# 96 instead of 128 token slots for each expert of a top-2-of-8 mixture

## The chip, the cores and the metric

The kernel runs on one core of one Trainium2 chip. The core has a matrix engine (PE in the profile, its weight loads in a row of their own, PEld), a vector engine (DVE), a scalar engine (ACT), a general engine (POOL) and 16 DMA engines that are fed by queues, here nearly all by that of SyncE (SP). The metric is device time in microseconds (us) of one launch, the median of several runs. Lower is better.

## What is computed

Two transformer layers over 256 latent tokens and 256 context tokens of width 1024. Layer 0 has retention and attention heads side by side and a dense feed-forward; layer 1 has latent attention and then, for the latent tokens alone, a top-2-of-8 mixture of experts. Only the mixture matters here:

```
t = h.reshape(b * n, d)                                     # 256 tokens, 1024 wide
logits = t @ router                                         # 8 experts
top_v, top_i = lax.top_k(logits, 2)
top_w = softmax(top_v)
gates = sum(one_hot(top_i, 8) * top_w[..., None], axis=1)   # two nonzeros a token
for e in range(8):
    out += gates[:, e:e+1] * ((silu(t @ w1[e]) * (t @ w3[e])) @ w2[e])   # w1, w3: 1024x3584, w2: 3584x1024
```

The reference multiplies all tokens with all experts. With the reference's inputs the router sends 65, 57, 65, 59, 82, 57, 65 and 62 tokens to the eight experts (counted on a CPU from the reference itself).

## The kernel before

All weights are f32 in HBM. For precision an operand is split into two parts of the matrix engine's f32r format, high and low, and a product is made of three matmuls: high times high, low times high, high times low. The split of a weight unit (128 x 2048 values, 1 MB) takes one ACT copy into a tile `uH` (line 103) and one DVE subtraction into a tile `uL` (line 104); both kinds have two buffers. The f32 originals come by DMA into a ring of some dozen 8 KB places (`uraw`, `xp`, `h0`, `a0`, `xn`, `raw`, ...), which the profile shows under those names.

Layer 0 and the attention of layer 1 take the first 820 us. Of the attention's tiles the rows below name `mk` and `mq`, plain f32 operands of a score product with 96 rows, `krx`, which is transposed in blocks of 96 columns, and `sil`, 32 columns of weights for the conditioning. Then `route` (one call for each of the two token tiles) computes norm, router logits, ranks, and for every token its slot at each of its experts (`pos`). `select` writes `S`, a 0/1 matrix of 128 tokens by 2 experts x 128 slots, by comparing `pos` with `iota`. `moe(0)` then does everything for the slots 0 to 127 of every expert:

- gather (`gather_step`, line 1589): for each pair of experts and each of four pairs of K tiles, eight matmuls with the tokens `xnH`, `xnL` as weights and `S` as the stream of 2 x 128 columns; then norm scale and shift (`mhf`, line 1603), then a split into `xe`, of 1024 x 128 for each expert. The gather of the next pair stands among the products of the odd expert before it.
- first products (line 1708): for each expert and each of seven column groups j of 512, `w1` and `w3` in two units each. Weights of a matmul are a 128 x 128 block of `xe` (K by slots), the stream is 512 columns of `uH` or `uL`. 48 matmuls a group.
- `ma` = silu times product (lines 1727, 1728), four transposes (line 1626) and a split into `aa`, slots in columns.
- second product (line 1631): blocks of `aa` as weights, 512 columns of `w2` as stream, 24 matmuls a group, summed over all j in two PSUM banks.
- at the end of an expert the gate and a split make `y` (line 1672), and `scatter` adds it to the token stream `rx` by the transpose `ST` of `S` (line 1686).

After `moe(0)` the largest token count of an expert is read into a register, and if it is over 128, `moe(1)` does the same for slots 128 to 255. It is not entered here. Within an engine the order of the instructions is set by a list scheduler that runs when the kernel is built; only calls in `keep_in_program_order` keep their written order.

Of the kernel before, what the change touches and what calls it, by code (L numbers as in the profile page):

```python
# [8 lines left out]
F32 = mybir.dt.float32  # L9
# [7 lines left out]
P = 128  # L17
# [6 lines left out]
NJ = ED // 512  # L24
MAGIC = float(0x5F3759DF)
# [3 lines left out]
class Split:  # L29
    """an operand in two float32r parts: H(k, cols) + L(k, cols), each [128, cols]"""  # L30
# [14 lines left out]
class SplitRow:  # L45
    """one column per K tile, the same for all tokens"""
# [12 lines left out]
def hybrid_kernel(ctx: ExitStack, tc: tile.TileContext, i, out):  # L59
# [3 lines left out]
    # ------------------------------------------------------------- pools  # L63
# [22 lines left out]
    # ------------------------------------------------------------- weight units of at most 1 MB  # L86
# [35 lines left out]
    def unit_rows(o, X, wh, wl, k0, kn, ktiles, ts_):  # L122
        """o [128 tok, n] += sum over the unit's K tiles of X[k, tok]^T w[k]"""
        for k in range(kn):
            mm(o, X.H(k0 + k, ts_), wh[:, k, :], k0 + k == 0, False)
            mm(o, X.L(k0 + k, ts_), wh[:, k, :], False, False)
        for k in range(kn):
            mm(o, X.H(k0 + k, ts_), wl[:, k, :], False, k0 + k == ktiles - 1)

    def rows_gemm(X, w, ktiles, c0, cn, toks, tags, kmax=4, w0=0):  # L130
        """psum[t] [128 tok, cn] = sum_k X[k, t]^T w[k, c0:c0+cn]"""
# [8 lines left out]
    def rows_pieces(X, w, c0, toks, evac):  # L140
        """one unit of all K tiles, 256 columns, as one piece per token tile"""
        ws = []

        def piece(t):
            if not ws:
                ws.extend(split_unit(w_src(w, 0, KD, c0, 256), (KD, 256)))
            ps = psum("mm")
            unit_rows(ps[:, :256], X, *ws, 0, KD, KD, tok(t))
            evac(t, ps)

        return [(24 * 256, lambda t=t: piece(t)) for t in toks]
# [5 lines left out]
    def block_cols(o, wh, wl, bs, X, cs):  # L157
        """o [128 features, tokens cs]"""
# [6 lines left out]
    def interleave(*lists):  # L165
        """emits lists of (cost, piece) side by side, each spread over the whole"""
# [9 lines left out]
    # ------------------------------------------------------------- helpers  # L176
    def rstd(ms, n, scale=None):
        """1/sqrt(scale*ms + EPS), [P, n] fp32"""
# [24 lines left out]
    def table(f):  # L203
        """the table of a function of ScalarE, ahead of its first use"""
# [9 lines left out]
    def bcast_into(t, reps):  # L214
        """vectors on every partition, each repeated r times"""
# [19 lines left out]
    # ------------------------------------------------------------- adaLN parameters  # L235
    class Ada:
        """columns 2048 r .. 2048 r + 2048; row 32 j + s of the result holds chunk j of stream s"""
# [66 lines left out]
    # ------------------------------------------------------------- norm, modulation, transposition  # L304
    def norm_rows(xr, pool, junk=None, tag="xn", act=()):
        """rows / rms(rows): two [128, D], in place if there is only room for junk"""
# [36 lines left out]
    # ------------------------------------------------------------- softmax attention, one head and query tile at a time  # L343
    def softmax_rows(ps, nk, scale, pool, sums, col, bufs=3):
        """exp(scale (s - max)) in a [128, nk] tile, its sum in sums[:, col]"""
# [8 lines left out]
    # ============================================================= start: streams, vectors, first modulation  # L354
    sil = const.tile([P, KD, 32], F32, tag="sil", name="sil")
    nc.gpsimd.memset(sil, 0.0)
    # the table of this function serves the first norms as well
# [32 lines left out]
    # silu(c), silu(c_ctx) as 32-wide stationary blocks per K tile (columns 0, 1 used)  # L390
# [4 lines left out]
    # ============================================================= layer 0  # L395
    # tiles of 8 KB that the parts after each other take over one by one
# [12 lines left out]
    # the first modulation streams through slots that later hold other things; part q of it is all that K tiles  # L409
    # 2 q and 2 q + 1 of the modulated rows need: row 32 j + s holds shift (j < 2) or 1 + scale of K tile 2 q + j % 2  # L410
# [54 lines left out]
    # ---- GQA query projection, K tile by K tile as the modulated rows appear  # L465
# [48 lines left out]
    # ---- constants of the attention parts: distances (3 x 384), rotary tables, gains  # L514
# [11 lines left out]
    # values: the two parts side by side, in the order high, low for the first key head and low, high for the second  # L526
# [22 lines left out]
    # queries, later values, of two token tiles each  # L549
# [7 lines left out]
    def gqa_pre(s):  # L557
        """normalised and rotated queries and keys; per head, both parts below each other"""
# [30 lines left out]
    # ---- GQA attention, two heads at a time  # L589
    # operand of the output projection: K tile 4 + g holds head g of both key heads, K tile hp two retention heads  # L590
# [47 lines left out]
    # ---- first stretch: gates and retention values with the GQA heads among them  # L638
# [8 lines left out]
    def rv_evac(u):  # L647
        def evac(t, ps):
            """less their mean: the group norm's mean is then zero"""
# [13 lines left out]
    def cols_chunks(w, c0, evacs):  # L663
        """a unit of 256 features, per 128 of them a list of pieces"""
# [52 lines left out]
    # queries of a token tile make room for its values  # L717
# [4 lines left out]
    # ---- retention in quadratic form, two heads at a time, transposed: [2 x 64 dims, 512 tokens]  # L722
# [5 lines left out]
    def ret_masks(hp):  # L728
        """decay by distance, within a stream (both directions, two at distance 0) and from latent to context tokens"""
# [57 lines left out]
    def ret_norm(hp):  # L787
        """group norm over each head: its scale goes into the gate"""
# [17 lines left out]
    # ---- output projection, column half by column half; K tiles of the GQA heads first  # L806
# [30 lines left out]
    # ---- second stretch: retention heads among the next heads' projections  # L837
# [54 lines left out]
    # the latent stream's norm under the context stream's last products  # L892
# [10 lines left out]
    # ---- SwiGLU, in three parts of the hidden width  # L903
# [34 lines left out]
    def ffn_down(part, s):  # L938
        """both column halves for one stream"""
# [10 lines left out]
    for part in range(2):  # L950
        A = new_A()
        f0, nf = PARTS[part]
        for b0 in range(0, nf, 2):
            if part == 0 and b0 == 0:
                # the latent stream first, while the context stream is still being normalised
# [20 lines left out]
    # ---- last part: latent stream first; layer 1 starts on it under the context stream  # L976
# [7 lines left out]
    def blk(n, s=1):  # L984
        """two blocks of one stream: the first, then the second product"""
# [36 lines left out]
    # keys and values of the two streams, queries (the first two take over what the latent stream's hidden rows leave)  # L1022
# [3 lines left out]
    def lora_T(rows, n, gname, X):  # L1026
        """rows transposed, times the gain"""
# [9 lines left out]
    def lora(ps, n):  # L1037
        """rms-normalised rows of ps[t][:, :n]"""
# [15 lines left out]
    def rope_rows(o, sincos, nh):  # L1054
        """o = o * cos + swapped(o) * sin; last axis 32"""
# [10 lines left out]
    def rope_keys(s):  # L1066
        """shared rotary keys of one stream"""
# [25 lines left out]
    def kv_rows(pp, s, tt, kr_, rs2=None):  # L1093
        """rs2: the factor of the rows of CK, where it is still to be applied, and its square"""
# [39 lines left out]
    def q_rows(pp, t):  # L1134
# [15 lines left out]
        # the gains of both sides of the plain part  # L1150
# [21 lines left out]
    # what the shift of the context stream adds to its keys and values  # L1172
# [39 lines left out]
    # ---- last products of the context stream; its norm is applied after the projection  # L1212
# [73 lines left out]
    # ============================================================= layer 1: latent attention  # L1286
# [18 lines left out]
    def mla_attend(t, hp, between):  # L1305
        """values of two heads side by side: [2 x 64 dims, 2 x 128 queries], of which the diagonal blocks count"""
# [17 lines left out]
        # 1 / sum of every query on all partitions  # L1324
# [18 lines left out]
    def w_out_gated(c):  # L1343
        """one column half of w_out times the gate of its columns"""
# [31 lines left out]
    iota = const.tile([P, 2, P], F32, tag="iota", name="iota")  # L1376
    nc.sync.dma_start(iota, bass.AP(tensor=i["iota"].tensor, offset=i["iota"].offset, ap=[[0, P], [P, 2], [1, P]]))
# [5 lines left out]
    def route(t, also=lambda n: None):  # L1383
        """the second norm of one token tile, applied after the router's products; also: what fills its waits"""
# [24 lines left out]
        # rank of every expert; equal logits in index order  # L1409
# [11 lines left out]
        # the slot of every token at each of its experts; others get a slot that no column has  # L1421
# [12 lines left out]
    def select(S, half, e, t):  # L1434
        """columns of the slots of two experts"""
        ins = DVE.tensor_tensor(S[:, t, :, :], iota[:, half, :].unsqueeze(1).to_broadcast([P, 2, P]),
                                pos[:, t, e:e + 2].unsqueeze(2).to_broadcast([P, 2, P]), op=ALU.is_equal)
# [3 lines left out]
    def gather_mm(ps, S, kp, ts):  # L1441
        for kk in range(2):
            o = ps[:, 256 * kk:256 * kk + 256]
# [8 lines left out]
    def gather_first(kp, tag):  # L1452
        """what the first token tile gives the first two experts, before the second tile is routed"""
# [13 lines left out]
    S0 = modp.tile([P, 2, 2, P], F32R, tag="adab", name="S0")  # L1467
# [27 lines left out]
    # the first expert's first weights are split, and what the first token tile gives is gathered, in the waits of the  # L1495
    # routing: quarters (part, unit, quarter) and column pairs by place
# [25 lines left out]
    # ============================================================= experts  # L1522
    mo = ctx.enter_context(tc.tile_pool(name="mo", bufs=1))
    # room that the first expert does not need yet takes weights as well
# [7 lines left out]
    def weights():  # L1532
        """softmax over the two largest logits, as weights of all experts"""
# [22 lines left out]
    def count():  # L1556
        """the largest number of tokens of an expert"""
# [254 lines left out]
```

## Time and profile before

| | |
|---|---|
| timed runs | 1838.48, 1840.38, 1842.13 us, median 1840.38 |
| profiled execution | span 1837.4 us from first to last instruction; no other time is recorded for it |
| mixture of experts | from about 841 us (first product) to 1830 us |
| busy share of the span | PE 98%, PEld 80%, DVE 76%, ACT 61%, DMA 74% |

PE busy is not PE at its peak: matmuls overlap in the record (one of 512 columns is recorded as 390 ns long, but the next one starts 227 ns after it). So the pace of PE is read from starts, or from the length of a run of matmuls, and not from the mean duration. A group row has its busy time, the mean duration of one in ns, and the idle time of the engine just before its instructions with what ended it. A timeline row has start, length, and the count of equal instructions that follow each other.

### The profile page before, as it was taken

Reading aid. Unit: us, or ns where it says so; the run is one execution under the profiler, and the core shown is the slowest. Engines: PE = TensorE matmul, PEld = TensorE weight load, DVE = VectorE, ACT = ScalarE, POOL = GpSimd, SP = SyncE. Lnnn points to the kernel's source line nnn. Section 1 sums busy time; section 2 is a strip of 40 time slices with the busy share of each in tenths; the row PEclk is TensorE's granted clock in tenths of the full one; section 3 lists DMA queues with packets and bytes.
Section 4 is the critical chain, followed back from the end, with each engine's and each line's share of the span. In section 5 each row is a group of like instructions: output and inputs, shape, how many; then the busy total and the mean of one; then the engine's idle time right before and its main releaser. Section 6 shows DMA issues by size and latency. Waiting matters only on the chain.

```text
span 1837.4 us, 23898 instructions
## 1 busy us (share of the span) xinstructions
PE 1793.4 (98%) x9410; PEld 1465.7 (80%) x9410; DVE 1398.4 (76%) x1739; ACT 1124.5 (61%) x1189; POOL 14.2 (1%) x24
## 2 busy tenths in 40 slices
PE   6999999999999999999999999999999999999997
PEld 5778668878779998677888888878878888788786
DVE  4787677334335677788889889898898888898987
ACT  4686543322223454567777877777777777777775
POOL 0000000000000000020000000000000000000000
PEclk9999999999999999999999999999999999999999
DMA  8444442343344566958998999999999999999992
GB/s 284 162 138 132 169 114 93 101 147 109 126 161 151 173 199 209 341 210 311 358 361 323 363 364 355 360 343 351 363 342 370 372 345 336 351 371 367 351 371 79
DMA packets 228729, 483.42 MB, mean 263 GB/s; under 512 B 11013, under 2 KB 65626, under 8 KB 223490
## 3 DMA queue, kind: packets, MB, share of 16 engines
q1 hardware_dynamic: 228416, 481.70, 74.0%
q8 instruction: 76, 1.25, 0.3%
q14 instruction: 43, 0.35, 0.1%
q10 hardware_dynamic: 194, 0.12, 0.0%
HBM read 480.74 MB, written 1.05 MB: 262 GB/s over the span
## 4 chain that ended last, share of the span: by engine, by line
PE 87%; DVE 7%; ACT 2%; DMA 2%; issue 1%; ACTq 0%; DVEq 0%
PE ps L84 81%; PE ps L212 4%; DVE uL L104 3%; PE ps L257 2%; DMA uraw<-in_l_w_in_dram 1%; ACT uH L103 1%; DVE rx L1686 0%; DVE y L104 0%; DMA xn<-in_l_exp_w_dram 0%; DMA rx<-in_x_dram 0%; PE ps L428 0%; DVE rst L193 0%; DVE yg L1672 0%; ACT st L103 0%; DVE stf L761 0%
## 5 line engine op out<-in xcount | busy, mean ns | idle before, releaser
L84 PE MATMUL ps<-uH,xe 128*128 128x512 f32 x1792 | 449.9, 392 | 1.2 <-ACT xe L103 0.9
L84 PEld LDWEIGHTS ps<-uH,xe 128*128 128x128 f32 x1792 | 334.0, 188 | 72.2 <-ACT uH L103 1.3
L104 DVE TENSOR_TENSOR uL<-uraw,uH 128x2048 fp32r<-128x2048 f32 (+3 forms) x126 | 276.2, 2193 | 136.8 <-ACT uH L103 128.9
L103 ACT CAST uH<-uraw 128x2048 fp32r<-128x2048 f32 (+3 forms) x126 | 231.1, 1835 | 205.5 <-PE ps L84 164.7
L84 PE MATMUL ps<-uL,xe 128*128 128x512 f32 x896 | 244.9, 393 | 5.6 <-DVE uL L104 5.5
L104 DVE TENSOR_TENSOR uL<-h,uH 128x2048 fp32r<-128x2048 f32 x95 | 217.3, 2290 | 23.2 <-ACT uH L103 21.0
L84 PE MATMUL ps<-uH,aa 128*128 128x512 f32 x896 | 222.4, 390 | 0.0
L103 ACT CAST uH<-h 128x2048 fp32r<-128x2048 f32 x95 | 181.8, 1916 | 59.7 <-PE ps L84 49.3
L84 PEld LDWEIGHTS ps<-uL,xe 128*128 128x128 f32 x896 | 165.7, 188 | 45.8 <-DVE uL L104 12.8
L84 PEld LDWEIGHTS ps<-uH,aa 128*128 128x128 f32 x896 | 168.1, 188 | 35.5 <-issue 0.5
L84 PE MATMUL ps<-h,uH 128*128 128x256 f32 (+1 forms) x1008 | 176.7, 327 | 0.0
L84 PEld LDWEIGHTS ps<-h,uH 128*128 128x128 f32 x1008 | 150.9, 190 | 21.9 <-issue 3.2
L104 DVE TENSOR_TENSOR uL<-a,uH 128x2048 fp32r<-128x2048 f32 x60 | 137.3, 2290 | 17.2 <-ACT uH L103 13.8
L104 DVE TENSOR_TENSOR uL<-raw,uH 128x2048 fp32r<-128x2048 f32 (+1 forms) x60 | 135.2, 2253 | 15.0 <-ACT uH L103 13.7
L103 ACT CAST uH<-raw 128x2048 fp32r<-128x2048 f32 (+1 forms) x60 | 113.2, 1887 | 36.7 <-PE ps L84 33.9
L103 ACT CAST uH<-a 128x2048 fp32r<-128x2048 f32 x60 | 114.8, 1916 | 33.3 <-PE ps L84 33.3
L84 PE MATMUL ps<-uL,aa 128*128 128x512 f32 x448 | 123.7, 397 | 0.0
L84 PEld LDWEIGHTS ps<-uL,aa 128*128 128x128 f32 x448 | 81.5, 188 | 15.5 <-DVE uL L104 0.5
L84 PE MATMUL ps<-h,uL 128*128 128x256 f32 (+1 forms) x504 | 92.6, 326 | 0.0
L84 PE MATMUL ps<-uH,a 128*128 128x512 f32 x352 | 88.2, 391 | 1.1 <-ACT uH L103 1.1
L104 DVE TENSOR_TENSOR uL<-xp,uH 128x2048 fp32r<-128x2048 f32 (+1 forms) x34 | 76.9, 2262 | 11.9 <-ACT uH L103 9.0
L84 PEld LDWEIGHTS ps<-h,uL 128*128 128x128 f32 x504 | 76.9, 190 | 7.8
(383 smaller groups left out, 2385.7 us busy)
## 6 DMA issues: line engine op xcount, KB each, us to landing
h<-in_l_exp_w_dram SPq DMA_DIRECT2D x94, 1024.0 KB
uraw<-in_l_exp_w_dram SPq DMA_DIRECT2D x60, 1024.0 KB
a<-in_l_exp_w_dram SPq DMA_DIRECT2D x60, 1024.0 KB
raw<-in_l_exp_w_dram SPq DMA_DIRECT2D x58, 1024.0 KB
uraw<-in_l_ffn_w_dram SPq DMA_DIRECT2D x38, 1024.0 KB
uraw<-in_l_ada_w_dram SPq DMA_DIRECT2D x34, 1024.0 KB
xp<-in_l_exp_w_dram SPq DMA_DIRECT2D x30, 1024.0 KB
xn<-in_l_exp_w_dram SPq DMA_DIRECT2D x30, 1024.0 KB
```

The source lines that it names most:

```text
L84: PE.matmul(o, l, r, start=start, stop=stop)
L103: h = ACT.copy(H, src)
L104: l = DVE.tensor_sub(L, src, H.bitcast(F32))
L212: PE.transpose(o, in_, ident[:in_.shape[0], :in_.shape[0]])
L257: PE.matmul(self.ps[32 * j:32 * j + 32, :], sil[:, self.k, :], raw[:, 512 * j:512 * j + 512], start=(self.k == 0), stop=(self.k == KD - 1) ...
```

## The change

Each expert has `CAP` = 96 slots. `S` has 2 x 96 columns, `xe` and `aa` have 96 columns a block, `ma`, `y` and `ST` have 96 partitions, and all products of an expert write 96 PSUM partitions. `moe(1)` now serves slots 96 to 191 and is entered if an expert has more than 96 tokens, and inside that branch a third copy, `moe(2)`, serves the rest. The table `iota` is filled with -1 beyond 255. Matmul count, streams of the weights, DMAs and splits of the weights are the same.

```diff
+CAP = 96
-    iota = const.tile([P, 2, P], F32, tag="iota", name="iota")
-    nc.sync.dma_start(iota, bass.AP(tensor=i["iota"].tensor, offset=i["iota"].offset, ap=[[0, P], [P, 2], [1, P]]))
+    iota = const.tile([P, 3 * CAP], F32, tag="iota", name="iota")
+    nc.gpsimd.memset(iota[:, 2 * P:], -1.0)
+    bcast_into(iota, [(i["iota"], 1, 2 * P)])
...
-        ins = DVE.tensor_tensor(S[:, t, :, :], iota[:, half, :].unsqueeze(1).to_broadcast([P, 2, P]),
-                                pos[:, t, e:e + 2].unsqueeze(2).to_broadcast([P, 2, P]), op=ALU.is_equal)
+        slots = iota[:, CAP * half:CAP * half + CAP]
+        ins = DVE.tensor_tensor(S[:, t, :, :], slots.unsqueeze(1).to_broadcast([P, 2, CAP]),
+                                pos[:, t, e:e + 2].unsqueeze(2).to_broadcast([P, 2, CAP]), op=ALU.is_equal)
...
-            o = ps[:, 256 * kk:256 * kk + 256]
+            o = ps[:, 2 * CAP * kk:2 * CAP * kk + 2 * CAP]
...
-                xe[e + ee] = xp.tile([P, 2, KD, P], F32R, tag=("a1", "a3", "h3")[(e + ee) % 3], name=nm("xe"))
+                xe[e + ee] = xp.tile([P, 2, KD, CAP], F32R, tag=("a1", "a3", "h3")[(e + ee) % 3], name=nm("xe"))
...
-                transpose(tp[:, tok(b)], a[:, tok(b)])
-            aa = mo.tile([P, 2, 4, P], F32R, tag="aa", bufs=2, name=nm("aa"))
-            split_to(aa[:, 0, :, :], aa[:, 1, :, :], v3(tp[:, :], 4))
+                transpose(tp[:, CAP * b:CAP * b + CAP], a[:, tok(b)])
+            aa = mo.tile([P, 2, 4, CAP], F32R, tag="aa", bufs=2, name=nm("aa"))
+            split_to(aa[:, 0, :, :], aa[:, 1, :, :], v3(tp[:, :4 * CAP], 4))
...
-                        mm(yps[ch], aa[:, 0, b, :], wh[:, k, cs], j == 0 and b == 0, False)
-                        mm(yps[ch], aa[:, 1, b, :], wh[:, k, cs], False, False)
+                        mm(yps[ch][:CAP, :], aa[:, 0, b, :], wh[:, k, cs], j == 0 and b == 0, False)
+                        mm(yps[ch][:CAP, :], aa[:, 1, b, :], wh[:, k, cs], False, False)
...
-                        unit_rows(ps, XE, wh, wl, k0, 4, KD, tok(0))
+                        unit_rows(ps[:CAP, :], XE, wh, wl, k0, 4, KD, slice(0, CAP))
...
-    with tc.If(cm > P):
+    with tc.If(cm > CAP):
         moe(1)
+        with tc.If(cm > 2 * CAP):
+            moe(2)
```

The scheduler keeps the order at most places and moves the gather by some rows. On PE, near the start of the second expert, where the first expert's results are scattered (`ps` is PSUM, `S` against `xnH` and `xnL` the gather, the numbers tell tiles apart), eight gather matmuls stood together, of which these are the last two:

```order
L84 MATMUL ps_9173<-S_9047,xnH 128x256
L84 MATMUL ps_9173<-S_9047,xnL 128x256
L84 MATMUL ps_9052<-uL_9056,xe_7968 128x512 x2
L84 MATMUL ps_9021<-y_8975,ST_8089 128x512 x2
L84 MATMUL ps_9052<-uL_9056,xe_7968 128x512 x2
L84 MATMUL ps_9052<-uH_9073,xe_7968 128x512 x8
```

After the change three of the eight stand there, of which these are the last two, and the other five 72 matmuls later:

```order
L85 MATMUL ps_9174<-S_9048,xnL 128x192
L85 MATMUL ps_9174<-S_9048,xnH 128x192
L85 MATMUL ps_9053<-uL_9057,xe_7969 96x512 x3
L85 MATMUL ps_9022<-y_8976,ST_8090 128x512 x2
L85 MATMUL ps_9053<-uL_9057,xe_7969 96x512
L85 MATMUL ps_9053<-uH_9074,xe_7969 96x512 x8
```

On DVE the splits that follow that gather step stood ahead of a weight split and of the split of `aa`:

```order
L104 TENSOR_TENSOR uL_9158<-xp_1561_9155,uH_9157 128x2048
L104 TENSOR_TENSOR xe_9050<-mhf_9182,xe_9050 128x256
L104 TENSOR_TENSOR xe_9051<-mhf_9182,xe_9051 128x256
L104 TENSOR_TENSOR uL_9193<-h_1567_9190,uH_9192 128x2048
L104 TENSOR_TENSOR aa_9152<-ps_9147,aa_9152 128x512
```

and now stand two weight splits later:

```order
L105 TENSOR_TENSOR uL_9159<-xp_1561_9156,uH_9158 128x2048
L105 TENSOR_TENSOR uL_9194<-h_1567_9191,uH_9193 128x2048
L105 TENSOR_TENSOR aa_9153<-ps_9148,aa_9153 128x384
L105 TENSOR_TENSOR uL_9212<-h_1570_9209,uH_9211 128x2048
L105 TENSOR_TENSOR xe_9051<-mhf_9183,xe_9051 128x192
L105 TENSOR_TENSOR xe_9052<-mhf_9183,xe_9052 128x192
```

The rows of DVE at the end of an expert (`yg`, `y`, `rx` among the weight splits) keep their order.

## Rows read from the trace of the kernel before

**Rows 1.** Busy time of each engine by stretch: us, then PE, PEld, DVE, ACT, POOL
```profile
900.00:1000.00 100.00, 100.00 (x457) 82.50 (x456) 91.67 (x59) 74.90 (x52) 0.00 (x0) 1.00 0.95 347
1300.00:1400.00 100.00, 98.94 (x447) 80.77 (x446) 89.16 (x55) 72.37 (x51) 0.00 (x0) 1.00 0.98 357
1700.00:1800.00 100.00, 98.99 (x443) 80.77 (x442) 90.11 (x54) 72.45 (x48) 0.00 (x0) 1.00 0.97 354
```
**Rows 2.** Waits between 900 and 1838 us: who for whom, us in total, times, longest
```profile
ACT uH L103 <- PE ps L84: 165.3, 236, 1.5
DVE uL L104 <- ACT uH L103: 78.8, 161, 1.4
PEld ps L84 <- DVE uL L104: 13.0, 19, 1.0
```
**Rows 3.** PE's groups from 841 us on, by form
```profile
L84 PE MATMUL ps<-uH,xe 128*128 128x512 f32 x1792 | 449.9, 392 | 1.2 <-ACT xe L103 0.9 <-DVE xe L104 0.3
L84 PE MATMUL ps<-uL,xe 128*128 128x512 f32 x896 | 244.9, 393 | 5.6 <-DVE uL L104 5.5
L84 PE MATMUL ps<-uH,aa 128*128 128x512 f32 x896 | 222.4, 390 | 0.0
L84 PE MATMUL ps<-uL,aa 128*128 128x512 f32 x448 | 123.7, 397 | 0.0
L212 PE MATMUL ps<-ident,ma 128*128 128x128 f32 x224 | 34.0, 272 | 0.0
L84 PE MATMUL ps<-y,ST 128*128 128x512 f32 x64 | 23.4, 412 | 1.5 <-ACT y L103 1.0 <-DVE y L104 0.5
```
**Rows 4.** Timeline of PE in a steady stretch: start us, us, instruction, count
```profile
1302.41 1.98 PE L84 MATMUL ps<-uH,xe 128*128 128x512 f32 x8
1304.22 1.07 PE L84 MATMUL ps<-uL,xe 128*128 128x512 f32 x4
1305.13 1.98 PE L84 MATMUL ps<-uH,aa 128*128 128x512 f32 x8
```
**Rows 5.** Timeline of PE and PEld in the first gather
```profile
832.88 0.97 PEld L84 LDWEIGHTS ps<-routS,tT 128*128 128x128 f32 x8
...
835.05 0.28 PE L84 MATMUL ps<-S,xnH 128*128 128x256 f32 x1
...
835.41 0.28 PE L84 MATMUL ps<-S,xnL 128*128 128x256 f32 x1
```
**Rows 6.** Tiles xe, ST, mk, S, krx, sil: duration ns min/median/max, first and last start, forms
```profile
L84 PEld LDWEIGHTS ps<-uH,xe x1792: 186/188/193, 841.8 to 1812.5; 128*128 128x128 f32 x200
L84 PE MATMUL ps<-y,ST x64: 387/392/505, 976.5 to 1829.1; 128*128 128x512 f32 x64
L84 PEld LDWEIGHTS ps<-mk,mq x64: 186/190/246, 764.7 to 816.0; 96*128 96x128 f32 x64
L84 PEld LDWEIGHTS ps<-S,xnH x64: 186/188/192, 832.3 to 1526.5; 128*128 128x128 f32 x64
L212 PEld LDWEIGHTS ps<-ident,S x16: 138/139/223, 833.7 to 1561.6; 128*128 128x128 f32 x16
L212 PEld LDWEIGHTS ps<-ident,krx x48: 122/126/129, 690.7 to 767.4; 128*96 128x96 f32 x48
L257 PEld LDWEIGHTS ps<-uraw,sil x240: 105/108/111, 73.8 to 783.5; 128*32 128x32 f32 x120
```
**Rows 7.** Timeline of PE, plain f32 matmuls of the attention
```profile
764.33 0.60 PE L212 MATMUL ps<-ident,krx 128*96 128x128 f32 x4
764.77 1.03 PE L84 MATMUL ps<-mk,mq 96*128 96x256 f32 x4
```
**Rows 8.** DVE's and ACT's instructions on tiles that shrink, as in 6
```profile
L103 ACT CAST xe<-mhf x32: 392/406/422, 841.3 to 1531.1; 128x256 fp32r<-128x256 f32 x32
L104 DVE TENSOR_TENSOR xe<-mhf,xe x32: 415/419/426, 842.1 to 1531.6; 128x256 fp32r<-128x256 f32 x32
L104 DVE TENSOR_TENSOR aa<-ps,aa x56: 678/684/692, 859.6 to 1817.8; 128x512 fp32r<-128x512 f32 x56
L1601 DVE TENSOR_SCALAR mhf<-ps,s,sh x4: 532/535/538, 840.8 to 842.5; 128x256 f32<-128x256 f32 x4
```
**Rows 9.** Timeline of PE at the end of the third expert
```profile
1219.93 0.39 PE L84 MATMUL ps<-y,ST 128*128 128x512 f32 x1
1220.77 1.21 PE L84 MATMUL ps<-uL,xe 128*128 128x512 f32 x4 [0.45 <-DVE uL L104]
```

More of the change, by code (lines that the diff above doesn't have):

```diff
@@ L1466, in hybrid_kernel @@
     sh2 = mod_shift(mod_T(row1), 2, "sh2_1")
-    S0 = modp.tile([P, 2, 2, P], F32R, tag="adab", name="S0")
+    S0 = modp.tile([P, 2, 2, CAP], F32R, tag="adab", name="S0")
     pairs = [(t, hp) for t in range(2) for hp in range(4)]
@@ L1572, in gather_begin @@
             else:
-                Ss[e] = modp.tile([P, 2, 2, P], F32R, tag="adab", name=nm("S"))
+                Ss[e] = modp.tile([P, 2, 2, CAP], F32R, tag="adab", name=nm("S"))
                 for t in range(2):
@@ L1582, in gather_S @@
                 for t in range(2):
-                    transpose(tp[:, tok(2 * ee + t)], Ss[e][:, t, ee, :].bitcast(F32))
+                    transpose(tp[:CAP, tok(2 * ee + t)], Ss[e][:, t, ee, :].bitcast(F32))
             for ee in range(2):
-                s = mo.tile([P, 256], F32R, tag="ST", bufs=4, name=nm("ST"))
-                ACT.copy(s, tp[:, 256 * ee:256 * ee + 256])
+                s = mo.tile([CAP, 256], F32R, tag="ST", bufs=4, name=nm("ST"))
+                ACT.copy(s, tp[:CAP, 256 * ee:256 * ee + 256])
                 STs[e + ee] = s
@@ L1598, in gather_step @@
                 k = 2 * kp + kk
-                o = ps[:, 256 * kk:256 * kk + 256]
+                o = ps[:, 2 * CAP * kk:2 * CAP * kk + 2 * CAP]
                 if tag and kk:
@@ L1606, in split @@
                 x_ = xe[e + ee]
-                split_to(x_[:, 0, 2 * kp:2 * kp + 2, :], x_[:, 1, 2 * kp:2 * kp + 2, :], hf[:, :, tok(ee)], pin)
+                split_to(x_[:, 0, 2 * kp:2 * kp + 2, :], x_[:, 1, 2 * kp:2 * kp + 2, :], hf[:, :, CAP * ee:CAP * ee + CAP], pin)
             split(0)
@@ L1616, in hf_tile @@
                 if kp % 2 == 0:
-                    spare.append(mo.tile([P, 2, 2, 256], F32, tag="aa", bufs=2, name=nm("mhf")))
+                    spare.append(mo.tile([P, 2, 2, 2 * CAP], F32, tag="aa", bufs=2, name=nm("mhf")))
                 return spare[-1][:, kp % 2, :, :]
-            return mo.tile([P, 2, 256], F32, tag="hf", name=nm("mhf"))
+            return mo.tile([P, 2, 2 * CAP], F32, tag="hf", name=nm("mhf"))
         spare, seconds = [], []
@@ L1646, in second @@
                         b = 2 * u + k
-                        mm(yps[ch], aa[:, 0, b, :], wl[:, k, cs], False, j == NJ - 1 and b == 3)
+                        mm(yps[ch][:CAP, :], aa[:, 0, b, :], wl[:, k, cs], False, j == NJ - 1 and b == 3)
         def second_last(e, j, aa, yps):
-            y = mo.tile([P, 2, D], F32R, tag="y", name=nm("y"))
+            y = mo.tile([CAP, 2, D], F32R, tag="y", name=nm("y"))
             for ch in range(2):
@@ L1656, in second_last @@
                     for b in range(n):
-                        mm(yps[ch], aa[:, 0, b0 + b, :], wh[:, b, :], False, False)
-                        mm(yps[ch], aa[:, 1, b0 + b, :], wh[:, b, :], False, False)
+                        mm(yps[ch][:CAP, :], aa[:, 0, b0 + b, :], wh[:, b, :], False, False)
+                        mm(yps[ch][:CAP, :], aa[:, 1, b0 + b, :], wh[:, b, :], False, False)
                     for b in range(n):
-                        mm(yps[ch], aa[:, 0, b0 + b, :], wl[:, b, :], False, b0 + b == 3)
+                        mm(yps[ch][:CAP, :], aa[:, 0, b0 + b, :], wl[:, b, :], False, b0 + b == 3)
                 y_parts(yps, (ch,), y)
@@ L1667, in y_parts @@
             if y is None:
-                y = mo.tile([P, 2, D], F32R, tag="y", name=nm("y"))
+                y = mo.tile([CAP, 2, D], F32R, tag="y", name=nm("y"))
             for ch in chs:
                 cs = slice(512 * ch, 512 * ch + 512)
-                g = mo.tile([P, 512], F32, tag="hf", name=nm("yg"))
-                DVE.tensor_mul(g, yps[ch], g2[ch])
+                g = mo.tile([CAP, 512], F32, tag="hf", name=nm("yg"))
+                DVE.tensor_mul(g, yps[ch][:CAP, :], g2[ch][:CAP, :])
                 split_to(y[:, 0, cs], y[:, 1, cs], g)
@@ L1725, in moe @@
                     pp.append(ps)
-                a = mo.tile([P, 512], F32, tag="a", name=nm("ma"))
-                tc.keep_in_program_order(ACT.activation(a, pp[0], AF.Silu))
-                DVE.tensor_mul(a, a, pp[1])
+                a = mo.tile([CAP, 512], F32, tag="a", name=nm("ma"))
+                tc.keep_in_program_order(ACT.activation(a, pp[0][:CAP, :], AF.Silu))
+                DVE.tensor_mul(a, a, pp[1][:CAP, :])
                 if e == 0 and j == 0:
```

## The prediction

> **What bounds the kernel now.** I read the windows first. In the mixture of experts PE is busy 99 to 100% of every stretch, at a granted clock of 1.00 (of 2.4 GHz), while DVE stands at 88 to 92% and ACT at 72 to 75% [rows 1]. DMA is also at 95 to 98% of its time, so the waits have to say which of the two binds. ACT waits 165 us for PE to give up `uH` buffers and DVE 79 us for ACT; PE's own loads wait 13 us for `uL` [rows 2], and no wait for a DMA is near that size. The stage is bound by PE, so the question is what a matmul with 96 instead of 128 columns of weights costs.
>
> PE's work there is 4032 expert products (1792 + 896 + 896 + 448) with 512 columns of stream each, 224 transposes of `ma`, 64 scatter matmuls [rows 3] and 128 gather matmuls. In a steady stretch twelve products go from 1302.41 to 1305.13 us [rows 4], that is 2.72 / 12 = 227 ns each. So the products take 4032 x 0.227 = 915 us of the 987 us from the first product's load at 841.8 to the last scatter at 1829.1 [rows 6]. Of the rest, some 20 us are waits, most at the ends of experts, where DVE falls behind by its extra work: there a product starts 0.84 us after the scatter matmul ahead of it, not 0.23 [rows 9].
>
> **What sets 227 ns.** 512 columns at 2.4 GHz are 213.3 ns, so 13.3 ns are over. Gather matmuls, with 256 columns, follow each other at (835.41 - 835.05) / 3 = 120 ns [rows 5], which is 106.7 + 13.3. The charge is thus one for each matmul, and not for each column of the stream; there is one weight load for each matmul. Plain f32 matmuls with the same kind of load (190 ns long, against 188 for the split operands [rows 6]) stream at half the rate: four with 256 columns take 1.03 us, the last of them 0.38, so (1.03 - 0.38) / 3 = 217 ns [rows 7] against 213.3 for two cycles a column. There the charge is 3 ns or less. I read this as a load that runs beside the stream, but takes some of its cycles when the stream runs at the full rate. A load gets shorter with its columns: 139 to 126 ns for transposes from 128 to 96 columns, 190 to 108 for plain f32 from 128 to 32 [rows 6]. So I take the charge to go with the columns of weights: 13.3 x 96/128 = 10.0 ns, a pace of 223.3 ns.
>
> The Trainium skill (TensorE: Matmul & The Clock Gate, section Back-to-back issue gap) gives an isolated matmul N / 2.4 + 2.5 ns, 216 ns for 512 columns, with no term for the columns of weights. The trace has 227, so that charge is not the page's. By the page's form, a charge that the weights' width does not change, products would gain nothing; that is the second case below.
>
> **The change part by part.**
>
> Products: 4032 x 3.3 ns = 13.4 us less, on the path, since PE binds. Bounds: 0 if the charge is fixed; on the other side the third case below. More than 13.4 is excluded as long as a load remains that is charged at all by its columns.
>
> Gather: 64 columns less of stream in 128 matmuls. The stream alone would give 80 + 13 = 93 ns; loads of 128 columns with hardly any stream go at (0.97 - 0.19) / 7 = 111 ns [rows 5], and the gather's weights keep 128 columns. I take 111: 128 x (120 - 111) = 1.2 us less. Bounds: 3.5 us less at 93 ns; and since no split matmul under 256 columns stands in the trace, the nearest row on the other side is plain f32, 0.85 ns a column [rows 7], 163 ns for 192 columns, 5.5 us more. I take the former, because 256 columns are far faster than that row.
>
> Transposes of `ma`: weights are 128 columns as before, the stream is 96 columns instead of 128. Now four transposes go at about 108 ns; 111 by the load. 224 x 3 ns = 0.7 us more; bound 0. The 16 transposes of `S` keep their 128 columns of stream.
>
> DVE and ACT: on DVE the split of `aa` takes 684 ns for 512 columns and that of `xe` 419 for 256 [rows 8], so 1.04 ns a column; 384 columns take some 551, 192 some 352; 56 x 0.13 + 32 x 0.07 = 9.7 us of DVE, about as much on ACT. Almost all of it lies beside PE. It counts only where DVE is behind, at the ends of seven experts: the burst there (`yg`, `y`, `aa`, `rx`) gets 0.13 us shorter, with the two `S` of a pair 0.27, about 1.3 us in all. Against it, PE comes to the same buffers sooner: 1.5% of some 12 us a burst, 0.18 us an expert, 1.3 us. I take 0 for the two, bounds -1.3 and +1.3. Without the cover of PE's products all 9.7 us would show.
>
> Before the first product the path runs over `S`, the gather and three `mhf` of 535 ns on DVE [rows 8]: 25% fewer columns, some 0.07 us each, and one split: 0.35 us less.
>
> The moved rows of gather and splits: the gather is done tens of microseconds before its expert needs `xe`, so a place 72 matmuls later costs nothing by itself. A step that stands among products adds the same 8 matmuls to PE wherever it stands. If DVE were late there, a `uL` would come late by at most the two splits that moved, 0.7 us, for three pairs 2 us; I take 0.
>
> DMA: the same bytes. If products get 1.5% faster the rate goes from about 357 to 362 GB/s over such windows; the busy share of 0.98 [rows 1] is no full queue, since no engine waits for it. The iota table's memset and its DMA stand far ahead of their use. The second branch is not entered, and the third lies inside it.
>
> Sum: -13.4 - 1.2 + 0.7 + 0 - 0.35 = -14.2 us. The profiled execution has a span of 1837.4, so 1823.2; the median of the timed runs is 3.0 us over that span, so **1826.2 us**, 0.8% faster. For this case alone the range is 1821 to 1831.
>
> **The rivals.**
>
> *The charge does not depend on the weights' width* (for: it is the same for 256 and 512 columns, and would be as well if it were the exchange of weights; against: plain f32 shows next to none with the same load). Then -0.8 us remain: 1839.5, no change that can be told.
>
> *The narrower load is dearer* (slower). The place is each of the 4032 products. 13.3 ns are 32 cycles for 128 columns, four columns a cycle. If that were a fast way of loading that only full 128 columns get, 96 columns would take 96 cycles, 40 ns, and a product 253 ns: 4032 x 26.7 = 108 us more, 1947. It decides from 1.1 ns a product on: at 228.1 ns the time is 0.2% over the median, with the other terms at -0.8. Against it: the recorded load of split operands is as long as plain f32's (188 and 190 ns [rows 6]), and loads of 96 columns stand in the trace, beside the stream as ever, with four transposes in 0.60 us [rows 7].
>
> The Trainium skill (same page, section Weight-path perf modes) says that fast weight load is on when the number of weights is 128 and the type is not FP32, and speaks so against this change. No run here shows whether f32r counts as FP32 there; the equal loads speak for it.
>
> *The gather at 192 columns falls to a slower rate*: at 163 ns for 192 columns the sum is -7.5 us instead of -14.2, 1832.9; at the whole 217 ns of that row for 256 columns, 128 x 97 = 12.4 us more, 1839.8.
>
> *The change doesn't do what it says*: an expert with more than 96 tokens lets `moe(1)` run, some 985 us more. The counts of the reference's inputs end at 82, and the branch for over 128 stayed untaken, so this has under 1%.
>
> **How the numbers follow.** The charge goes with the width, and all else as summed: 53%, 1821 to 1831. The charge is fixed: 25%, 1836 to 1842. The gather is slower: 10%, 1833 to 1852 by either charge. The load is dearer: 8%, from 1844 on. It falls by more than its share, below 1820: 4%. A change of 0.2%, 3.7 us, is about what a measurement of this kernel can tell from none. Faster than 1836.7: 53 + 4, half of the gather's 10, and a tenth of the fixed one's 25, 0.64. Slower than 1844.1: the dearer load, 2 of the gather's, and some of the fixed one's with bad moves, 0.13. The same: 0.23. The range 1820 to 1843 leaves out the dearer load, the far end of the gather and the below-1820 case, some 17%.
>
> **What would show it.** Starts in a steady stretch: twelve products in 2.68 us (right), 2.72 (fixed), 3.04 (dearer). PEld's loads of `xe` and `aa` shorter than 188 ns by 13 to 27. Eight gather matmuls in a row at 111 ns (93, 163). The transposes of `ma` four in about 0.44 us to the next start. PE's busy share unchanged, its waits for `uL` of the same size. If the time falls with products at 227 ns, the gain is from waits, and my reading of the charge is wrong.

## The result, and the profile after

The changed kernel takes 1850.22 us (median of 4 runs, 1848.94 to 1852.48), the kernel before 1840.0 in the same comparison (4 runs, 1838.48 to 1842.13). The ratio is 1.0059, with a 95% interval from 1.0047 to 1.0072: slower by 10 us, where 14 us faster were predicted, and outside the range. The profiled execution has a span of 1847.8 us.

PE is the bound as before. These are the windows that answer to [rows 1] (busy us of PE, PEld, DVE, ACT, POOL, then the granted clock, DMA share and GB/s):

```profile
900.00:1000.00 100.00, 99.92 (x446) 70.06 (x445) 89.38 (x57) 71.56 (x49) 0.00 (x0) 1.00 0.94 341
1300.00:1400.00 100.00, 98.87 (x446) 68.94 (x445) 86.60 (x56) 71.81 (x54) 0.00 (x0) 1.00 0.96 345
1700.00:1800.00 100.00, 98.85 (x440) 68.53 (x439) 87.51 (x55) 70.34 (x48) 0.00 (x0) 1.00 0.98 360
```

PE is as busy as it was, at the same clock of 1.00, and gets through fewer instructions in each of the three (446, 446 and 440, before 457, 447 and 443), while its loads take 69 to 70 us of a stretch, not 81 to 82. The waits that answer to [rows 2], from 900 us on, show who is late:

```profile
ACT uH L104 <- PE ps L85: 196.3, 246, 1.9
DVE uL L105 <- ACT uH L104: 95.8, 180, 1.3
...
PEld ps L85 <- DVE uL L105: 8.9, 15, 0.9
```

ACT and DVE wait longer for PE (196 and 96 us, before 165 and 79), and PE's loads less for them (8.9, before 13.0). So PE has become slower at the same work. The timeline of PE in a steady stretch answers to [rows 4]:

```profile
1306.20 2.03 PE L85 MATMUL ps<-uH,xe 128*96 128x512 f32 x8
1308.07 1.09 PE L85 MATMUL ps<-uL,xe 128*96 128x512 f32 x4
1309.00 2.00 PE L85 MATMUL ps<-uH,xe 128*96 128x512 f32 x8
1310.84 1.09 PE L85 MATMUL ps<-uL,xe 128*96 128x512 f32 x4
1311.76 0.63 PE L85 MATMUL ps<-uH,aa 128*96 128x512 f32 x2
```

Twelve products take 2.80 and then 2.76 us, before 2.72. Over all gaps under 260 ns from the start of a product to that of the next product or scatter matmul, from 870 us on, the mean is 231.7 ns (3767 gaps), before 227.5 (3739). This mean is called the pace below. PE's groups by form, from 843 us on, answer to [rows 3]; the loads come from the same view of the whole span:

```profile
L85 PE MATMUL ps<-uH,xe 128*96 128x512 f32 x1792 | 458.8, 396 | 3.2 <-ACT uH L104 3.2
...
L213 PE MATMUL ps<-ident,ma 96*128 96x96 f32 x224 | 28.3, 245 | 0.0
```
```profile
L85 PEld LDWEIGHTS ps<-uH,xe 128*96 128x96 f32 x1792 | 286.2, 162 | 125.5 <-ACT uH L104 5.5
...
L213 PEld LDWEIGHTS ps<-ident,ma 96*128 96x128 f32 x224 | 25.4, 140 | 9.5
```

The recorded load of a product did get shorter, 162 for 188 ns, and yet products follow each other more slowly. Transposes of `ma` went the other way: their load is as long as before (140, before 139), and they follow each other at 83 ns instead of 108.

Two things lie ahead of the steady part. The last matmul of the router starts 1.9 us later than before (836.50, not 834.64 us), with the work up to there unchanged but for the table of `iota`; some 500 matmuls in, in layer 0, it is late already (74.3 us, before 72.0). This point moves from profile to profile (834.63 to 838.14 us in e1 to e8, e10, e13 and e14 below), and I put it down to no part of the change. (In e9, e11 and e12 it lies at 841.45, 837.10 and 839.99; their unused tile moves tiles of layer 0 too.) And in this profile twelve gather matmuls and the first eight products run at half the clock:

```profile
843.79 0.41 PE L85 MATMUL ps<-S,xnL 128*128 128x192 f32 x1
844.00 3.62 PE L85 MATMUL ps<-uH,xe 128*96 128x512 f32 x8
847.42 1.25 PE L85 MATMUL ps<-uL,xe 128*96 128x512 f32 x4
```

The products start 427 ns apart, which is 512 columns at 1.2 GHz, and the gather matmuls 213 ns instead of 111; the granted clock of 842 to 850 us is 0.64. PE had waited ahead of this, 0.82 us for `uH` among the gather's matmuls. The products cost 8 x 0.2 = 1.6 us in this profile; the slow gather matmuls fall into a time in which PE waits for `xe` at the full clock (in e1 1.1 us from the last of them to the first product). It comes and goes: of the kernels below, e3 and e5 have the same order and a wait of the same length there (1.11 us from one start to the next), and e3 shows no such product, e5 ten.

From the 25th product to the last scatter matmul it is 989.4 us (851.28 to 1840.70), before 981.1 (847.98 to 1829.08): 8.3 more. The pace gives 4008 x 4.15 = 16.6, transposes 224 x -25 = -5.6, the 96 gather matmuls in that part 96 x -12.6 = -1.2; what is left, -1.5, I take to be shorter waits, since ACT and DVE have more time; no run shows it by itself.

### The profile page after: what moved, and what is told of

It is laid out like the page before. It is cut to its first block, busy times and chain, and to the rows that moved or that the text cites. A ratio compares the mean times of both kernels' runs of the same rounds, so it can differ in the third digit from the quotient of the medians.

```text
span 1847.8 us, 23895 instructions
## 1 busy us (share of the span) xinstructions
PE 1803.3 (98%) x9410; PEld 1356.4 (73%) x9410; DVE 1389.7 (75%) x1739; ACT 1115.3 (60%) x1189; POOL 14.2 (1%) x25
## 4 chain that ended last, share of the span: by engine, by line
PE 86%; DVE 7%; ACT 3%; DMA 3%; issue 1%; SPq 0%; ACTq 0%; DVEq 0%
PE ps L85 80%; PE ps L213 3%; DVE uL L105 3%; PE ps L258 2%; ACT uH L104 2%; DMA uraw<-in_l_w_in_dram 1%; DMA uraw<-in_l_w_out_dram 0%; DVE rx L1690 0%; DMA rx<-in_x_dram 0%; DVE y L105 0%; DMA raw<-in_l_exp_w_dram 0%; DVE yg L1676 0%; DMA uraw<-in_l_exp_w_dram 0%; DVE rst L194 0%; DMA xn<-in_l_exp_w_dram 0%
## 5 line engine op out<-in xcount | busy, mean ns | idle before, releaser
L85 PE MATMUL ps<-uH,xe 128*96 128x512 f32 x1792 | 458.8, 396 | 3.2 <-ACT uH L104 3.2
L85 PEld LDWEIGHTS ps<-uH,xe 128*96 128x96 f32 x1792 | 286.2, 162 | 125.5 <-ACT uH L104 5.5
L85 PE MATMUL ps<-uL,xe 128*96 128x512 f32 x896 | 247.8, 396 | 3.5 <-DVE uL L105 3.2
L85 PE MATMUL ps<-uH,aa 128*96 128x512 f32 x896 | 226.3, 394 | 0.0
L85 PEld LDWEIGHTS ps<-uL,xe 128*96 128x96 f32 x896 | 143.2, 161 | 67.6 <-DVE uL L105 8.7
L85 PEld LDWEIGHTS ps<-uH,aa 128*96 128x96 f32 x896 | 144.4, 161 | 64.5 <-issue 0.5
L85 PE MATMUL ps<-uL,aa 128*96 128x512 f32 x448 | 123.5, 397 | 0.0
L85 PEld LDWEIGHTS ps<-uL,aa 128*96 128x96 f32 x448 | 70.4, 161 | 27.6 <-DVE uL L105 0.2
```

The source lines that it names most:

```text
L85: PE.matmul(o, l, r, start=start, stop=stop)
```

## The experiments

Two facts of the built program matter (the addresses are the program's; the traces show none). In the kernel before, a block of `xe` or `aa` (one K tile's weights) is 512 bytes long in each partition, and so is the distance from one to the next. In the changed kernel both are 384. And `iota` is 128 bytes longer there, so that `uH`, `uL`, `xe`, `aa` and all that is allocated behind it start 64 bytes past a multiple of 512, and not 448. In the table, "position" is where blocks start against the rows of `uH` and `uL` that stream meanwhile, modulo 256 bytes. Each ratio is to the kernel before in the same comparison (medians of 1838.6 to 1840.0 us).

| kernel | columns loaded | distance, bytes | position | ns a product | us | ratio to before, 95% interval |
|---|---|---|---|---|---|---|
| before | 128 | 512 | 0 | 227.5 | | |
| changed | 96 | 384 | 0, 128 in turn | 231.7 | 1850.2 | 1.0059 (1.0047 to 1.0072) |
| e1 | 96 | 512 | 0 | 230.1 | 1843.5 | 1.0025 (1.0014 to 1.0036) |
| e2 | 128 | 384 | 0, 128 in turn | 233.0 | 1856.4 | 1.0098 (1.0081 to 1.0114) |
| e3 | 128 | 512 | 0 | 227.4 | 1835.2 | 0.9972 (0.9962 to 0.9981) |
| e4 | 64 | 256 | 0 | 230.1 | 1861.7 | 1.0123 (1.0106 to 1.0139) |
| e5 | 128 | 512 | 0 | 227.9 | 1837.7 | 0.9989 (0.9978 to 1.0000) |
| e6 | 128 | 512 | 0 | 227.8 | 1835.8 | 0.9975 (0.9960 to 0.9990) |
| e7 | 96 | 512 | 0 | 230.1 | 1842.8 | 1.0017 (1.0006 to 1.0029) |
| e8 | 128 | 512 | 0 | 227.7 | 1835.4 | 0.9975 (0.9963 to 0.9986) |
| e9 | 128 | 512 | 128 | 232.5 | 1859.6 | 1.0107 (1.0078 to 1.0136) |
| e10 | 128 | 512 | 0 (256) | 227.7 | 1835.2 | 0.9974 (0.9960 to 0.9987) |
| e11 | 128 | 512 | 64 | 233.4 | 1859.1 | 1.0104 (1.0075 to 1.0134) |
| e12 | 96 | 512 | 128 | 231.4 | 1850.9 | 1.0058 (1.0035 to 1.0080) |
| e13 | 112 | 512 | 0 | 230.1 | 1846.7 | 1.0054 (1.0037 to 1.0071) |
| e14 | 128 | 512 | 0 | 227.4 | 1834.5 | 0.9982 (0.9972 to 0.9992) |

**e1 to e4: width or distance.** e1 keeps 96 columns and gives the blocks their old distance:

```
-xe[e + ee] = xp.tile([P, 2, KD, CAP], F32R, ...)
+xe[e + ee] = xp.tile([P, 2, KD, P], F32R, ...)      # split and products use [..., :CAP]
...
-aa = mo.tile([P, 2, 4, CAP], F32R, ...)
+aa = mo.tile([P, 2, 4, P], F32R, ...)
```


> The blocks of xe and aa lie 128 columns (512 bytes) apart as in the kernel before, but products still load 96 columns of each. (The third pass, which is never entered, is left out, for its 128 bytes of iota are needed.) Theory A, the load of 96 columns itself is dearer: products stay at 231.7 ns, the time at 1850. Theory B, blocks 384 bytes apart are read badly: products at 227.5 ns, 4032 x 4.2 = 17 us less than the changed kernel, 1833.

e2 keeps the distance and loads 128 columns:

```
+class Wide:
+    def H(self, k, cs=None):
+        return self.t[:, CAP * k:CAP * k + P]
...
```


> The blocks lie 96 columns (384 bytes) apart as in the changed kernel, but each product loads 128 columns, its own 96 and the first 32 of the next block, whose 32 rows of output nobody reads. (The third pass, never entered, is left out.) Theory A, the load of 96 columns is dearer: products back at 227.5 ns, 17 us less than the changed kernel, 1833, and that is 7 us under the kernel before, by the transposes of ma (224 at 82 instead of 108 ns, 5.8 us) and the gather (128 x 10 ns). Theory B, the 384 bytes: products at 231.7 ns, 1850.

e3 undoes both:

```
+nc.gpsimd.memset(xe[e + ee][:, :, :, CAP:].bitcast(F32), 0.0)
...
-unit_rows(ps[:CAP, :], XE, wh, wl, k0, 4, KD, slice(0, CAP))
+unit_rows(ps, XE, wh, wl, k0, 4, KD, tok(0))        # aa in the same way
```


> Both undone: blocks 128 columns apart, 128 columns loaded, the last 32 set to zero by GpSimd; gather, transposes, splits, y and scatter stay at 96 slots. (The third pass, never entered, is left out.) Theories A and B both say 227.5 ns a product and 1833. If it is the writes of GpSimd that matter or the transposes do not give their 5.8 us back, 1840 or above.

e4 changes the size (and, as e1 to e3, has `iota` at its old length and no third pass):

```
-CAP = 96
+CAP = 64
...
-with tc.If(cm > CAP):
+with tc.If(cm > 2 * CAP):
```


> The changed kernel with 64 slots instead of 96, and the branch taken only from 129 tokens on, so the tokens of an expert beyond its 64th are left out of the result. Blocks are 256 bytes apart. If the charge of a load went with its columns, as the prediction had it, products would be at 213.3 + 6.7 = 220 ns, 4032 x 11.7 = 47 us under the changed kernel, 1803. If any load that is not 128 columns wide is dear by the same amount: 231.7 ns, some 1848. If only a block stride that is no multiple of 256 bytes is bad: 227.5 ns or less, 1833 or less.

Steady stretches of PE's timeline, first e1, then e2, e3 and e4:

```profile
1304.37 2.00 PE L85 MATMUL ps<-uH,xe 128*96 128x512 f32 x8
1306.21 1.08 PE L85 MATMUL ps<-uL,xe 128*96 128x512 f32 x4
1307.13 2.00 PE L85 MATMUL ps<-uH,aa 128*96 128x512 f32 x8
```
```profile
1307.25 2.04 PE L96 MATMUL ps<-uH,xe 128*128 128x512 f32 x8
1309.13 1.09 PE L96 MATMUL ps<-uL,xe 128*128 128x512 f32 x4
1310.06 2.03 PE L96 MATMUL ps<-uH,xe 128*128 128x512 f32 x8
```
```profile
1303.31 1.98 PE L85 MATMUL ps<-uH,aa 128*128 128x512 f32 x8
1305.13 1.07 PE L85 MATMUL ps<-uL,aa 128*128 128x512 f32 x4
1306.03 1.98 PE L85 MATMUL ps<-uH,aa 128*128 128x512 f32 x8
```
```profile
1302.60 2.00 PE L85 MATMUL ps<-uH,aa 128*64 128x512 f32 x8
1304.44 1.08 PE L85 MATMUL ps<-uL,aa 128*64 128x512 f32 x4
1305.36 2.00 PE L85 MATMUL ps<-uH,aa 128*64 128x512 f32 x8
1307.29 0.46 PE L213 MATMUL ps<-ident,ma 64*128 64x64 f32 x4
```

Twelve products take 2.76, 2.81, 2.72 and 2.76 us. Neither theory holds alone: e1 wins back 1.6 of the 4.2 ns by the distance, e3 the other 2.7 by the width. The distance is worse for wide loads (5.6 ns, e2 against e3) than for narrow ones (1.6). e3 is also faster than the kernel before. e4 has the pace of e1 with a third fewer columns, so the charge does not go with the columns. That it is slower still has its cause elsewhere: its transposes have 64 rows, and by the starts a product is then followed by a transpose after 328 ns instead of 231, and the last transpose by a product after 152 instead of 28, 56 times, some 12 us. Its scatter matmuls have 64 rows too: one starts 327 ns after a product (e1: 234), and the next product 423 ns after it (e1: 235), some 10 us in all by the sums of these gaps.

**e5 to e8: where the blocks lie.** Only the length of `iota` changes, from e3 (e5, e6, e8) and from e1 (e7), and moves all that lies behind it:

```
-iota = const.tile([P, 2 * P], F32, ...)
+iota = const.tile([P, 160], F32, ...)               # e6: 144, e8: 112
```


> The kernel of e3 (128 columns loaded, blocks 512 bytes apart), with iota 160 instead of 256 numbers long, so that every tile allocated behind it starts 64 bytes past a multiple of 512, as in the changed kernel, and not at 448, as in the kernel before and in e1 and e3. (The further passes, never entered, have the wrong slots, here and in the next three.) Theory A', what counts is where in memory a block starts: in e2 half of the blocks start 192 bytes past a multiple of 256, like those of e3 (227 ns a product), half 64 past one, and its mean was 233 ns, so all at 64 give 240 ns and 51 us more than e3, 1886. Theory B', what counts is the distance between blocks: 227 ns, 1835.

> The same with iota 144 long: every tile behind it starts at a multiple of 512 bytes. Theory A', the start of a block counts: if the start need only keep the 512 bytes within as few lines as may be, this is the best place: 227 ns or less, 1835 or less; if it is near to 64 that is bad, between 227 and 240. Theory B', the distance counts: 227 ns, 1835.

> The kernel of e1 (96 columns loaded, blocks 512 bytes apart), every tile 64 bytes past a multiple of 512. In e1 all blocks start at 448 and a product takes 230.1 ns; in the changed kernel half of them start 64 past a multiple of 256, half 192 past one, and it takes 231.7. Theory A': all at 64, so 230 + 2 x 1.6 = 233.3 ns, 13 us over e1, 1857. Theory B': 230 ns, 1843.

> The kernel of e3 with iota 112 long: every tile behind it starts 384 bytes past a multiple of 512. Theory A': between 448 (227 ns) and 320, which is bad if 64 is and 256 bytes are the period: 227 to 240 ns, 1835 to 1886. Theory B': 227 ns, 1835.

Theory A' fell: from 64, 0 and 384 bytes past a multiple of 512, products keep their 227.7 to 227.9 and 230.1 ns. Timelines of e5 and e7, twelve products in 2.72 and 2.76 us:

```profile
1303.59 1.98 PE L85 MATMUL ps<-uH,xe 128*128 128x512 f32 x8
...
1306.31 1.98 PE L85 MATMUL ps<-uH,aa 128*128 128x512 f32 x8
```
```profile
1303.01 2.00 PE L85 MATMUL ps<-uH,xe 128*96 128x512 f32 x8
...
1305.77 2.00 PE L85 MATMUL ps<-uH,aa 128*96 128x512 f32 x8
```

The longer `iota` of the change is thus harmless. But here the streams had moved with the weights, and so position against the stream remained, beside distance.

**e9 to e12: position against the stream.** An unused tile ahead of `xe` and `aa`, behind `uH` and `uL`, moves the one against the other (e9 to e11 from e8; e12 from e7, with the gap of e9 and the `iota` of e8):

```
 xp = ctx.enter_context(tc.tile_pool(name="xp", bufs=1))
+gap = xp.tile([P, 32], F32, tag="gap", name="gap")   # e10: 64, e11: 16
+nc.gpsimd.memset(gap, 0.0)
```


> The kernel of e8 (128 columns loaded, blocks 512 bytes apart) with 128 bytes of unused memory between uL and xe, so that every block of xe and aa starts 128 bytes further within 512 than the rows of uH and uL that stream meanwhile; in e1, e3 and e5 to e8 the two agree. Theory C, a load collides with the stream unless the two agree within 512 bytes: in e2 a quarter of the loads agree, and its mean of 233.3 ns against 226.7 puts the others at 235.5 on average, so some 235 ns a product, 33 us over e8, 1868. Theory D, the distance between one loaded block and the next counts: 227 ns, 1835.

> The same with 256 bytes between. Theory C: as above, some 235 ns and 1868, or 227 if 256 bytes are the period of the collision (then e9 has 240 ns and 1889). Theory D: 227 ns, 1835.

> The same with 64 bytes between, which no kernel so far had. Theory C: between 227 and 240 ns, above 227 if any difference counts. Theory D: 227 ns, 1835.

> 96 columns loaded from blocks 512 bytes apart (e7), with 128 bytes between uL and xe as in e9. Theory C: in the changed kernel a quarter of the loads agree with the stream, and 231.7 ns against the 230.1 of e1 and e7 puts the others at 232.2, so some 232 ns, 9 us over e7, 1851. Theory D: 230 ns, 1843.

Timelines of e9, e10, e11 and e12:

```profile
1302.41 2.02 PE L85 MATMUL ps<-uH,aa 128*128 128x512 f32 x8
1304.27 1.09 PE L85 MATMUL ps<-uL,aa 128*128 128x512 f32 x4
1305.20 2.02 PE L85 MATMUL ps<-uH,xe 128*128 128x512 f32 x8
```
```profile
1302.80 1.98 PE L85 MATMUL ps<-uH,aa 128*128 128x512 f32 x8
1304.62 1.07 PE L85 MATMUL ps<-uL,aa 128*128 128x512 f32 x4
1305.52 1.98 PE L85 MATMUL ps<-uH,aa 128*128 128x512 f32 x8
```
```profile
1304.37 2.03 PE L85 MATMUL ps<-uH,xe 128*128 128x512 f32 x8
1306.24 1.10 PE L85 MATMUL ps<-uL,xe 128*128 128x512 f32 x4
1307.17 0.49 PE L213 MATMUL ps<-ident,ma 96*128 96x96 f32 x4
```
```profile
1307.85 2.02 PE L85 MATMUL ps<-uH,xe 128*96 128x512 f32 x8
1309.71 1.09 PE L85 MATMUL ps<-uL,xe 128*96 128x512 f32 x4
1310.64 2.01 PE L85 MATMUL ps<-uH,xe 128*96 128x512 f32 x8
```

Theory C holds, with 256 bytes as good as none, and D falls as the only cause. The distance stays at 512, and twelve products take 2.79 us with 128 bytes between, 2.72 with 256, and 2.80 with 64. The sizes were off: 232.5 and 233.4 ns, not 235 or 240. e12 shows the same for 96 columns, 231.4 after 230.1 (in the stretch shown twelve in 2.79 us, in e7 2.76); all of its blocks are out of position, and it is about where the changed kernel is with half of them (231.7). Nor is e2's 233.0 the mean of 227.4 and 232.5. So blocks 384 bytes apart, whose position changes from load to load, cost as much as a wrong position that stays, or more; whether the change of position or the distance itself makes the rest, these runs do not separate.

**e13 and e14: the two wrong terms by themselves.** e13 is e1 with `CAP = 112`. e14 is the kernel before with `ma` of 96 rows:

```
-transpose(tp[:, tok(b)], a[:, tok(b)])
+transpose(tp[:, 96 * b:96 * b + 96], a[:, tok(b)])
...
+nc.gpsimd.memset(aa[:, :, :, 96:].bitcast(F32), 0.0)
...
-a = mo.tile([P, 512], F32, tag="a", name=nm("ma"))
+a = mo.tile([96, 512], F32, tag="a", name=nm("ma"))
```


> The kernel of e1 with 112 slots instead of 96: products load 112 columns from blocks 512 bytes apart, in agreement with the stream. Theory E, any load under 128 columns pays the same 8 cycles more (64 columns in e4 and 96 in e1 both had 230.0 to 230.1 ns): 230 ns a product; the transposes of ma stream 112 columns, 112 x 0.85 = 95 ns, 224 x 12 = 2.7 us more than e1, the gather up to 1 us more, so some 1847. Theory F, the loss grows with the columns left out and only happens to agree in e1 and e4: between 226.7 and 230.1, some 228.5 ns, 1841.

> The kernel before, with one part of the change alone: ma has 96 rows, so its transposes stream 96 columns (the last 32 columns of aa are set to zero by GpSimd; products load 128 columns, the gather keeps 256; the result is the reference's as long as no expert has more than 96 tokens). If the transposes are bound by their stream of plain f32 (108 to 83 ns, 224 times): 5.6 us less than before, 1834; nearly all of what e3 gains. If they were bound by their load, as the prediction had it: 0 to 1 us more, 1840.

With 112 columns the mean is 230.1, that of 64 and 96 columns, as theory E had it. Yet the mean is a mixture: stretches of 228.9 and of 233 ns alternate, as the windows of 25 us show (228.9 from 1175 to 1225, 232.7 from 1525 to 1550), while e1 stays between 229.9 and 230.4 throughout. One stretch of each kind, twelve products in 2.75 and in 2.80 us:

```profile
1182.95 1.99 PE L85 MATMUL ps<-uH,aa 128*112 128x512 f32 x8
...
1185.70 1.99 PE L85 MATMUL ps<-uH,aa 128*112 128x512 f32 x8
```
```profile
1302.63 2.03 PE L85 MATMUL ps<-uH,xe 128*112 128x512 f32 x8
...
1305.43 2.03 PE L85 MATMUL ps<-uH,xe 128*112 128x512 f32 x8
```

So neither theory is shown for 112 columns: the faster stretches are near theory F's 228.5, the mean is E's. What holds is that every window of 25 us is above the 227.4 ns of 128 columns. The recorded load is in between (175 ns). In e14 the transposes' group reads:

```profile
L212 PE MATMUL ps<-ident,ma 96*128 96x96 f32 x224 | 28.2, 245 | 0.0
L212 PEld LDWEIGHTS ps<-ident,ma 96*128 96x128 f32 x224 | 25.1, 140 | 7.5
```

It comes out 0.18% faster (1834.5 against 1838.6), 4.1 us of the 5.6 expected. In the profiles, from the 25th product to the last scatter matmul, it is 975.4 us against 981.1, 5.7 less, as much as 224 x 25 ns. e3 has 976.2 there: the transposes carry its gain.

## Why the prediction was wrong, step by step

**The charge goes with the columns of weights.** This is the step that failed: "13.3 x 96/128 = 10.0 ns, a pace of 223.3 ns". That the charge is one for each matmul no run put to the test; that it shrinks with the load was wrong. It rose, by 2.7 ns where blocks keep their position against the stream (e3 to e1), and by 1.6 more in the changed kernel (e1 to changed). The term was -13.4 us and measured 4032 x 4.15 = +16.7. Two rows had suggested it: narrower loads are shorter in the record [rows 6], which is still true (188, 175, 162 ns for 128, 112 and 96 columns), and plain f32 products show next to no charge. Neither says what a load takes from a stream at the full rate, and no row of before had a narrower load beside such a stream.

**The blocks' place in memory** stood in no term and no rival. Their distance was in the diff, 512 to 384 bytes. It costs 1.6 ns a product, 6.7 us by the medians of e1 and the changed kernel.

**The rival that the narrower load is dearer** had the place and the sign, and 231.7 ns is beyond the 228.1 from which it was to decide. Its price, 26.7 ns, was six times what came, and ten times what the width alone cost. It had 8%. The Trainium skill (TensorE: Matmul & The Clock Gate, section Weight-path perf modes) grants the fast weight load only to 128 weights that are not FP32. That products with loads of 64, 96 and 112 columns are all slower than with 128 agrees with such a rule for f32r, but the recorded load of 128 columns is the longest (188 ns, 162 for 96); that this mode is the cause no run shows.

**Transposes of `ma`.** Predicted 0.7 us slower, measured 5.6 faster. "111 by the load" was wrong: 108 ns are 128 columns of plain f32 at 0.85 ns a column, the price of [rows 7], and 96 columns would be 82; they measured 83. The row with the answer was used for the gather and not here. e14 shows the term by itself.

**Gather.** Predicted 111 ns, measured, from 870 us on, 111 as the median and 107.6 in the mean, before 117 and 120.2: by the means 128 x 12.6 = 1.6 us less, 1.2 predicted. (The 120 of the prediction came from one place; two gaps of some 200 ns are in the mean of before.) The rival of a slower rate fell.

**Waits of DVE and ACT** were put at 0, within 1.3 us. What the terms leave over is -1.5. **The routing** was to be 0.35 us shorter from the last router matmul to the first product; it is 7.50 us, before 7.15, with the half clock in it; in e1, at the full clock there, 7.04. **DMA** was right: no wait for it is near the size of those shown (2.4 us in total for the largest of them, from 900 us on), at 0.94 to 0.98 of its time. **The extra passes** were not entered.

The sum with measured terms is 16.6 - 5.6 - 1.2 - 1.5 = +8.3 from the 25th product to the last scatter matmul, +1.4 from the router to the 25th product (the half clock, most of it), +1.9 by the later start and -1.2 after the last scatter matmul: 10.4, the difference of the spans.

**What stays open:** why a load under 128 columns slows a stream, and why 112 columns alternate between two paces; why a load 256 bytes off the stream is as good as one at the same place, and one 64 or 128 bytes off is not. The runs show that it is so, not how. A product that loads 96 columns also writes 96 PSUM partitions instead of 128, and no run moves the one without the other, so the 2.7 ns belong to the two together.

## What to carry to other kernels

Here, where PE binds, fewer columns of weights saved nothing by themselves: keep the load at 128 columns and shrink the stream, or the operands that are streamed in plain f32 (as the transposes were), and price each by the row that has its kind of stream. Blocks of weights were best at the stream's own place, modulo 256 bytes, and so at a distance that keeps them there; a padded tile costs memory, a dense one cost 1.6 to 5.6 ns in each of 4032 products here. Of this change, the version to keep is e3 or e14: 128 columns loaded at a distance of 512 bytes, `ma` with 96 rows, 0.28% and 0.18% faster than the kernel before. As they ran, e3 has no pass for slots from 192 on and e14 none for slots 96 to 127 (with up to 82 tokens an expert neither is needed); for other inputs these have to be served again.

## What the runs showed of the hardware

- The pace of back-to-back f32r products of 512 columns depends on where the loaded block lies against the stream: with loads of 128 columns 227.7 ns at the same place (e8) or 256 bytes off (e10), 232.5 at 128 (e9) and 233.4 at 64 (e11). Moving both together changes nothing (e5 to e8).
- Loads of 64, 96 and 112 columns make a mean of 230.1 ns all three (with 112 columns a mixture of 228.9 and 233), against 227.4 for 128, although their records are shorter (134, 162 and 175 ns, against 188).
- Transposes with 64 rows of weights among products with 128 cost some 97 ns on the way in and 124 on the way out (e4); those with 96 rows do not (231 and 28 ns in the changed kernel). Scatter matmuls with 64 rows among such products cost some 93 ns on the way in and 188 on the way out (e4 against e1).
